# Twelve slots a window in place of fourteen, a third operand buffer, and a first pair whose preparation is spread, in a hybrid RWKV-7 and attention encoder

## The chip, the cores and the metric

The kernel runs on one core of one Trainium2 chip. The metric is the device time of one execution in microseconds (us), as the median of several runs. Engines are called by the names of the profile: PE multiplies matrices, DVE and ACT do elementwise work, POOL helps a little, SP issues the transfers. Each engine works through its own list of instructions in order and waits, where it must, for another engine's semaphore.

## The reference, cut to what matters

Two layers (DEPTH 2) over 256 tokens (T) of width 2048. In each, the normalised input goes through one projection, whose columns feed a bidirectional RWKV-7 time mixer with 16 heads of 64 and a windowed attention with 16 heads; the two, each under its own gate, go through an output projection and are added to the input.

```python
proj = jnp.einsum('btd,dc->btc', h, w_in[l])
rw_in = bidir_token_shift(rw_in, shift_mu[l])          # u + mu0*(prev-u) + mu1*(next-u)
...
kk = kk * lax.rsqrt(jnp.maximum(jnp.sum(kk * kk, -1, keepdims=True), 1e-24))
...
def step(S, inp):                                      # for each head, each direction
    r_t, w_t, k_t, v_t, kk_t, a_t = inp
    s_kk = jnp.einsum('bhvk,bhk->bhv', S, kk_t)
    S = (S * w_t[:, :, None, :] - s_kk[..., None] * (a_t * kk_t)[:, :, None, :]
         + v_t[..., None] * k_t[:, :, None, :])
    return S, jnp.einsum('bhvk,bhk->bhv', S, r_t)
...
bonus = bonus + jnp.sum(rh * kd * rkf, -1, keepdims=True)
mu = jnp.mean(y, -1, keepdims=True)                    # then variance, norm, bonus * v, gate
...
x = x + jnp.einsum('btc,cd->btd', mix, w_out[l])
```

## The kernel before, in words

**The stream.** The input projection of a layer is a stream `S` of steps. A step is three matmuls of 128x256 (L286, L287, L288): weights and input are split into a high and a low part (XH and XL for the input, `hi` by ACT at L216 and `lo` by DVE at L218 for the weights), and a step multiplies high by high, low by high and high by low. Sixteen steps make a tile of 128 columns in PSUM (`pm`), which DVE and ACT take out with the token shift (L413 to L416: `u`, `kr`, `vg`). The output projection is such a stream too, with MH and ML as its input. `S.run(n)` writes n steps; behind them weights are prepared ahead.

**The chains.** Beside the stream, the sixteen heads are worked on in eight pairs (NP = 8, `p`). The recurrence is brought into chunks of 64 tokens (NC = 4), so that it needs small matrix products. Three generators, each cut into stages by `yield`, write a pair's work:

- `scan_p` prepares: decay and learning rate by the matmuls `pza` (L648 to L650), a sum over each head of the squared key (`pk`), exponentials, the reciprocal `kd`, the operands BK and MV, and a second sum over the head for the bonus (`pbn`, of an operand `km` that has the tag `lw`). `head_sums` (L654) writes both sums; the bonus `bv` comes from the second.
- `scan_i` builds the chunks' matrices (`pg` L746, `ge` L752, AB, AL), transposes (`pt` L769 and L777, taken out by ACT as `bt` L782 and `suv` L787), and inverts a unit triangular matrix in levels: `tv` and `tt` begin as the unit matrix (L816), then `pq`, QF, `pd` and masked copies (L837 to L857), and a last step `pf`, `q`, `pn`, `vf` (L863 to L882).
- `scan_b` runs the state over the chunks: `pcc` L902, `rh` L904, L915, then `suv` by ACT L920 and DVE L927, L925, and the outputs `py` (L909 and L932). Behind the last chunk come the norm (`ysq` by ACT L943, `yv` DVE L944 and POOL L945, `ysq` with the mean removed by DVE at the helper's line L231, L952 by PE, `t` L954) and MH and ML, the operand of the output projection.

The helper at L231 writes many DVE and ACT instructions, so its line stands for many places; they are told apart by their tiles. PSUM has eight banks: two for `pm`, two (`ps_c`) for `pcc` and `py`, and two buffers of two banks that all other small products share (`pza`, `pk`, `pbn`, `pg`, `pt`, `pq`, `pd`, `pf`, `pn`).

**The windows.** A layer's projection is cut into thirteen windows of 64 steps. `window` cuts its 64 steps into SLOTS slots; in a slot it first runs the stages that tables place there (STAGE_P, STAGE_I, STAGE_B, and ATT for attention in the last windows), then its share of the stream's steps, four or five of them. A pair enters one window after another: in window `w`, `scans(w)` runs the preparation of pair w-1, the inverse of w-2 (its end in w-3's table), and the state of w-3 (its end of w-4). From window 4 to window 7 all chains are under way at once; the projection is followed by 256 steps of output projection.

**What sets the order.** On PE the order is as written: stage by stage and step by step. The other engines' lists are ordered by a scheduler from priorities (PRIO_B, PRIO_LO, and the helpers PA and PV, which put instructions in turn with the chains). Buffers are had by tag; where a tag has two buffers, the third pair's write waits for the first pair's last reader.

Of the kernel before, what the change touches and what calls it, by code (L numbers as in the profile page):

```python
# [9 lines left out]
F32 = mybir.dt.float32  # L10
F32R = mybir.dt.float32r
F16 = mybir.dt.float16
# [9 lines left out]
T = 256  # L22
DEPTH = 2
RW = 1024
NKT = D // 128
# [5 lines left out]
NC = T // CHUNK  # L31
# [9 lines left out]

SLOTS = 14
STAGE_P = [4, 5, 6, 7, 8, 9, 10, 11, 13]
STAGE_I = (list(range(SLOTS)), [0, 1])
STAGE_B = (list(range(1, 14)), [1, 2, 3, 4])
ATT = [
    [4, 11],
    [1, 3, 6, 8, 11, 13],  # L50
    [0, 2, 5, 7, 8, 10, 12, 13],
]
PRIO_B = 95
PRIO_LO = 40
# [75 lines left out]
def hybrid_trunk_kernel(ctx, tc, xT, wi, wv, wo, par, fing, dup, iup, sink, pos, cst, out):  # L130
    nc = tc.nc
    V, A, G, PE, SY = nc.vector, nc.scalar, nc.gpsimd, nc.tensor, nc.sync

    def pool(name, bufs, **kw):
        return ctx.enter_context(tc.tile_pool(name=name, bufs=bufs, **kw))
# [3 lines left out]
    wrp = pool("wrp", 3)  # L139
    wsp = pool("wsp", 2)  # L140
    sp = pool("sp", 1)
    big = pool("big", 4)
# [12 lines left out]
    def st(tag, shape, dt=F32, bufs=1):  # L155
        return sp.tile([128, *shape], dt, tag=tag, name=tag, bufs=bufs)
# [7 lines left out]
    half = (slice(0, 64), slice(64, 128))  # L164
# [9 lines left out]
    def bigt(dt, name):  # L174
        return big.tile([128, NKT, T], dt, tag="big", name=name)

    def x_split(XH, XL, x, k, l):
        g = G0[:, k : k + 1] if l == 0 else PR[:, l, P_NG + k : P_NG + k + 1]
# [45 lines left out]
    class InTurn:  # L224


        def __init__(self, engine):
            self.engine = engine
# [66 lines left out]

    first_w = wrp.tile([128, 1024], F32, tag="raw", name="raw")
    G0 = cp.tile([128, NKT], F32, name="G0")
    X0 = bigt(F32, "X0")
# [73 lines left out]

    def window(n, *gens, groups=SLOTS):

        done = 0
        for i in range(groups):
            for g, at in gens:
                for _ in range(at.count(i)):
                    if g.__name__ == "scan_b":
                        with tc.high_priority(offset=PRIO_B):  # L380
                            next(g, None)
                    else:
                        next(g, None)
            upto = n * (i + 1) // groups
            S.run(upto - done)
            done = upto
# [198 lines left out]
    def queue_output(l):  # L585

        L = layers[l]
        last = l + 1 == DEPTH

        def tile_of(k):  # L590
            xs = []

            def begin():
                xs.append(st("vg", [T], bufs=8))
                SY.dma_start(out=xs[0], in_=L.xin[:, k, :])

            def evac(pm):
                if last and k == 0:
                    L.X2 = bigt(F32, "X2")
                x = L.X2[:, k, :] if last else xs[0]  # L600
                V.tensor_tensor(x, pm, xs[0], op=ALU.add)
                to = end if last else layers[l + 1]
                if k == 0:
                    to.norm = Norm()
                    to.acc = st("acc", [T])
                    if not last:
                        to.XH, to.XL = bigt(F32R, "XH"), bigt(F32R, "XL")
# [24 lines left out]
    def layer(l):  # L632
        L = layers[l]
        prm = lambda o, j: PR[:, l, o + j : o + j + 1]
        dpm = lambda o, j: DP[:, l, o + j : o + j + 1]
        L.MH, L.ML = MH, ML = bigt(F32R, "MH"), bigt(F32R, "ML")

        def mix_split(j, y, g2):
            mf = st("mf", [T])
            V.scalar_tensor_tensor(mf, y, 0.5, g2, op0=ALU.mult, op1=ALU.mult)  # L640
            A.activation(MH[:, j, :], mf, AF.Copy)
            V.tensor_tensor(ML[:, j, :], mf, MH[:, j, :].bitcast(F32), op=ALU.subtract)

        order = (list(range(NC)), list(range(NC - 1, -1, -1)))
        cs = lambda c: slice(c * 64, (c + 1) * 64)
# [6 lines left out]
        def head_sums(o, x):  # L652
            for r in half:
                PE.matmul(o[r, 0:T], bones[r, r], x[r, 0:T], start=True, stop=True)  # L654
# [3 lines left out]
        def scan_p(p, t):  # L658
# [60 lines left out]
            PC = st("pc", [2, NC], bufs=3)  # L719
            PA.activation(PC[:, 0, :], PP[:, 0, :, 63], AF.Copy)  # L720
            PA.activation(PC[:, 1, :], PP[:, 1, :, 0], AF.Copy)
            yield


# [7 lines left out]
            t.update(BK=BK, MV=MV, PC=PC, bv=bv)  # L732
            yield


        def scan_i(p, t):
            VV, BK, MV = t["v"], t["BK"], t["MV"]
            flat = lambda x: x.rearrange("p d c j -> p (d c) j")
            GE = st("ge", [2, 2, NC, 2, 64], bufs=2)
            GE = [GE[:, h] for h in range(2)]  # L740
            GEd = lambda d: pick(GE[0], every, d * NC * 128, [2 * NC * 128, 2], [128, NC], [1, 128])
            for d in range(2):
# [30 lines left out]
            BT = st("bt", [2, 2, 3, 64], bufs=2)  # L773
            for d in range(2):
                for i in range(3):
                    for h in range(2):
# [3 lines left out]
                            ident[half[h], half[h]],  # L780
                        )
            A.activation(BT.rearrange("p h d i j -> p h (d i j)"), pt2[:, :, 0:384], AF.Copy)  # L782
            SUV = st("suv", [2, NC, 2, 64], bufs=2)
            t["SUV"] = SUV
            for h in range(2):
                for q in range(2):
# [24 lines left out]


            TC = st("tv", [2, NC, 64], F16)
            TT = st("tt", [2, NC, 64], F16)
            for x in (TC, TT):
                V.tensor_copy(flat(x), EYE.unsqueeze(1).to_broadcast([128, 2 * NC, 64]))  # L816
# [69 lines left out]
        def scan_b(p, t):  # L886
            GE, MV, BT, SUV, PC, bv = (t[n] for n in ("GE", "MV", "BT", "SUV", "PC", "bv"))


            pyt = ps_c.tile([128, 512], F32, tag="y", name="py")  # L890
            py = pyt[:, 0:256].rearrange("p (c j) -> p c j", j=64)
            for i in range(NC):
                ci = [order[d][i] for d in range(2)]

# [24 lines left out]
                for h in range(2):  # L919
                    A.activation(here(h), pc[half[h], 1], AF.Copy)  # L920
                yield
                if i < NC - 1:
# [110 lines left out]
        def attend():  # L1033

            scores(0)
            yield
            flip(0)
            scores(1)
            yield
            for j in range(8):  # L1040
                values(j)
                if j < 6:
                    scores(j + 2)
                yield
                if j < 7:
                    flip(j + 1)
                    yield

        for w in range(NP + 2):
            window(64, *scans(w), *([(setup_, [2, 5])] if l == 0 and w == 0 else []))  # L1050
        att = attend()
        window(64, *scans(NP + 2), (att, ATT[0]))
        window(64, *scans(NP + 3), (att, ATT[1]))
# [6 lines left out]
    V.memset(QF, 0.0)  # L1060
    L0 = layers[0]
    L0.norm = Norm()
    L0.XH, L0.XL = bigt(F32R, "XH"), bigt(F32R, "XL")
    for k in range(NKT):
        x_split(L0.XH, L0.XL, X0[:, k, :], k, 0)
        S.run(1)
# [113 lines left out]
```

## Time and profile before

| | |
|---|---|
| median of three runs | 1224.29 us (1222.6 to 1225.03) |
| profiled execution | 1220.4 us, span 1218.6 |
| mean granted PE clock | 0.992 |
| layer 0: projection's 13 windows | 27.77 to 518.91 us |
| layer 0: output projection | 518.91 to 623.83 us |
| layer 1: projection's 13 windows | 623.83 to 1113.19 us |
| a steady window (4 to 7 of a layer) | 42.07 us |

The windows' borders are found in the trace by counting the stream's matmuls. A row of the timeline has the start in us from the span's start, the duration, the engine, line and operation, and what is written from what. A row of the groups has the count, then the busy time and the mean of one in ns, then the idle time ahead with what ended most of it. A row of waits has the engine and line, what it waited for, and the sum, the number and the longest of the waits.

### The profile page before, as it was taken

How to read it: one execution, taken by the hardware profiler on the slowest of the kernel's cores; microseconds unless marked ns; L12 is line 12 of the kernel's file. 1: busy time of each engine (PE TensorE's matmuls, PEld its weight loads, DVE VectorE, ACT ScalarE, POOL GpSimd, SP SyncE). 2: the span in 40 equal slices, each digit the busy share in tenths (PEclk: the TensorE clock that was granted, in tenths of full speed). 3: DMA queues.
4: the chain of work that ended last, by engine and by line, in shares of the span. 5: the costliest groups of instructions: out<-in, count | busy, mean ns of one | idle time of the engine just before them, and what ended most of it. 6: DMA issues, size and time to landing. Idle time of an engine off the chain costs nothing. (4 is left out here: it accounts for less than half of the span.)

```text
span 1218.6 us, 38161 instructions
## 1 busy us (share of the span) xinstructions
PE 1177.0 (97%) x16204; PEld 1092.3 (90%) x16204; DVE 929.5 (76%) x2067; ACT 747.6 (61%) x1840; POOL 19.1 (2%) x23
## 2 busy tenths in 40 slices
PE   7989999999999999999999899999999999999996
PEld 6978998999898889999999788989999888899996
DVE  7978878888877668866677788878887866786554
ACT  6656665766666557655555556766676565675553
POOL 0000000000000000000000000000000000000000
PEclk9999999999999999999999999999999999999998
DMA  7533233323323433477654333233233334345653
GB/s 252 177 129 125 95 112 111 107 96 116 119 89 102 134 111 132 141 242 237 205 189 163 111 121 114 86 107 126 90 112 106 115 101 133 125 142 177 208 191 123
DMA packets 60411, 166.72 MB, mean 137 GB/s; under 512 B 7728, under 2 KB 22736, under 8 KB 60240
## 3 DMA queue, kind: packets, MB, share of 16 engines
q1 hardware_dynamic: 60240, 164.27, 40.5%
q8 instruction: 127, 2.08, 0.7%
q14 instruction: 44, 0.36, 0.1%
HBM read 157.43 MB, written 4.19 MB: 133 GB/s over the span
## 5 line engine op out<-in xcount | busy, mean ns | idle before, releaser
L286 PE MATMUL pm<-XH,hi 128*128 128x256 f32 x1664 | 497.0, 299 | 8.1 <-ACT XH L179 5.9
L216 ACT ACTIVATE hi<-raw 128x512 fp32r<-128x512 f32 x560 | 328.4, 624 | 247.8 <-PE pm L287 173.6
L288 PE MATMUL pm<-XH,lo 128*128 128x256 f32 x1664 | 470.1, 282 | 3.2 <-DVE lo L218 3.2
L287 PE MATMUL pm<-XL,hi 128*128 128x256 f32 x1664 | 469.7, 282 | 0.1
L218 DVE TENSOR_TENSOR lo<-raw,hi 128x512 fp32r<-128x512 f32 x560 | 368.5, 687 | 89.8 <-ACT hi L216 83.0
L286 PEld LDWEIGHTS pm<-XH,hi 128*128 128x128 f32 x1664 | 315.7, 190 | 33.8 <-issue 13.4
L288 PEld LDWEIGHTS pm<-XH,lo 128*128 128x128 f32 x1664 | 316.2, 190 | 4.5 <-DVE lo L218 4.0
L287 PEld LDWEIGHTS pm<-XL,hi 128*128 128x128 f32 x1664 | 316.5, 190 | 0.7 <-DVE XL L180 0.7
L286 PE MATMUL pm<-MH,hi 128*128 128x256 f32 x512 | 144.0, 281 | 0.0
L287 PE MATMUL pm<-ML,hi 128*128 128x256 f32 x512 | 143.8, 281 | 0.0
L288 PE MATMUL pm<-MH,lo 128*128 128x256 f32 x512 | 143.8, 281 | 0.0
L286 PEld LDWEIGHTS pm<-MH,hi 128*128 128x128 f32 x512 | 96.6, 189 | 0.8 <-issue 0.8
L287 PEld LDWEIGHTS pm<-ML,hi 128*128 128x128 f32 x512 | 96.6, 189 | 0.0
L288 PEld LDWEIGHTS pm<-MH,lo 128*128 128x128 f32 x512 | 96.6, 189 | 0.0
L920 ACT ACTIVATE suv<-pcc 64x128 f32<-64x128 f32 x128 | 34.2, 267 | 20.4 <-PE pq L847 14.4
L856 DVE CAST_PREDICATED tv<-LV,pd 128x256 f16<-128x256 uint8 x80 | 34.5, 431 | 13.6 <-PE pd L855 13.1
L849 ACT ACTIVATE QF<-pq 128x256 f16<-128x256 f32 x80 | 30.9, 386 | 20.8 <-PE pq L847 20.0
L752 DVE TENSOR_TENSOR ge<-pg,C 128x1024 f32<-128x1024 f32 x32 | 39.1, 1222 | 5.0 <-PE pg L746 5.0
L904 ACT ACTIVATE rh<-pcc 128x128 f32<-128x128 f32 x64 | 17.5, 273 | 35.3 <-PE pcc L902 34.9
L1005 ACT ACTIVATE mv<-mv,mx 128x257 f32<-128x257 f32 x64 | 31.8, 502 | 11.6 <-DVE mx L1002 11.6
L746 PE MATMUL pg<-mv,bk 64*128 64x128 f32 x512 | 37.2, 285 | 0.0
L857 DVE CAST_PREDICATED tt<-LV,pd 128x256 f16<-128x256 uint8 x80 | 34.1, 426 | 0.0
(240 smaller groups left out, 1849.9 us busy)
## 6 DMA issues: line engine op xcount, KB each, us to landing
raw<-wi SPq DMA_DIRECT2D x207, 512.0 KB, 3.4
raw<-wo SPq DMA_DIRECT2D x64, 512.0 KB, 3.8
raw<-wv SPq DMA_DIRECT2D x8, 512.0 KB, 3.2
rrot<-u SPq DMA_DIRECT2D x80, 32.0 KB, 1.9
vg<-xT SPq DMA_DIRECT2D x16, 128.0 KB, 5.2
xd<-vg SPq DMA_DIRECT2D x16, 128.0 KB, 2.4
vg<-xd SPq DMA_DIRECT2D x16, 128.0 KB, 3.5
g<-dup SPq DMA_DIRECT2D x16, 97.0 KB
```

Source lines behind the costliest of these rows:

```text
L216: A.activation(hi[:, q], raw[:, q], AF.Copy)
L218: V.tensor_tensor(lo[:, q], raw[:, q], hi[:, q].bitcast(F32), op=ALU.subtract)
L286: PE.matmul(pm, wh, rh[:, kk, :], start=(kk == 0), stop=False)
L287: PE.matmul(pm, wh, rl[:, kk, :], start=False, stop=False)
L288: PE.matmul(pm, wl, rh[:, kk, :], start=False, stop=(kk == 15))
L746: PE.matmul(pg[:, h, c * 128 : (c + 1) * 128], BK[half[h], d, c, 1 - h : 3 - h, :].rearrange("p s j -> p (s j)"), MV[half[h], d, c].rearra ...
L752: V.tensor_tensor(GEd(d), pg.rearrange("p h (c x) -> p h c x", c=NC), gm[d].unsqueeze(1).unsqueeze(1).to_broadcast([128, 2, NC, 128]), op= ...
L849: A.activation(t_sub(QF), flat4(pq[:, :, 0:128]), AF.Copy)
L856: V.copy_predicated(t_sub(TC), t_mask, flat4(pd[:, :, 0:128]))
L857: V.copy_predicated(v_sub(TT), v_mask, flat4(pd[:, 0, 128:384].rearrange("p (d x) -> p d x", d=2)))
L920: A.activation(here(h), pc[half[h], 1], AF.Copy)
L1005: A.activation(Sc[:, h, q, 0:257], Sc[:, h, q, 0:257], AF.Exp, scale=0.125, bias=mx[:, q : q + 1], accum_out=den[:, q : q + 1])
```

## The change

A window has 12 slots (of five or six steps) in place of 14, and all tables are written anew. The inverse runs over twelve slots and the first four of the next window. The state scan runs from slot 3 to 11 and then from slot 0 to 7 of the next window, where before it had 1 to 13 and 1 to 4. `scan_p` has two more yields, so that its two head sums are stages of their own, which `scans` puts ahead of the inverse in their slot (6 and 11). The first pair of a layer has tables of its own (STAGE_P0), which spread its preparation over windows 0, 1 and 2; before, all of it was in window 1. GE, BT and SUV get a third buffer, used by pairs with p % 3 == 2: it lies in the second halves of MH and ML, which are free until the last pairs. The second unit matrix (`tt`) is copied a stage later, and `py` is allocated behind the first yield of `scan_b`.

```diff
-SLOTS = 14
-STAGE_P = [4, 5, 6, 7, 8, 9, 10, 11, 13]
-STAGE_I = (list(range(SLOTS)), [0, 1])
-STAGE_B = (list(range(1, 14)), [1, 2, 3, 4])
+SLOTS = 12
+STAGE_P = (([6, 11], [4, 5, 6, 7, 8, 8, 9, 10, 11]),)
+STAGE_P0 = (([], [10, 11]), ([3], [3, 4, 5, 7, 9]), ([3], [1, 3]))
+STAGE_I = (list(range(SLOTS)), [0, 1, 2, 3])
+STAGE_B = (list(range(3, SLOTS)), list(range(8)))
...
-        L.MH, L.ML = MH, ML = bigt(F32R, "MH"), bigt(F32R, "ML")
+        L.MH, L.ML = MH, ML = Halves(F32R, "MH", "mh").more(), Halves(F32R, "ML", "ml").more()
...
+        spare = [x.half(1, F32).rearrange("p k t -> p (k t)") for x in (MH, ML)]
+        def third(p, n, tag, off, shape, dt=F32):
+            if p % 3 < 2:
+                return st(tag, shape, dt, bufs=2)
+            w = int(np.prod(shape))
+            names = " ".join(f"a{i}" for i in range(len(shape)))
+            x = spare[n][:, off : off + w]
+            return x.rearrange(f"p ({names}) -> p {names}", **{f"a{i}": v for i, v in enumerate(shape)})
...
             head_sums(pk, sq)
+            yield
...
             head_sums(pb, km)
-            bv = st("bv", [T], bufs=3)
+            yield
+            t["bv"] = bv = st("bv", [T], bufs=3)
...
-            GE = st("ge", [2, 2, NC, 2, 64], bufs=2)
+            GE = third(p, 0, "ge", 0, [2, 2, NC, 2, 64])
...
-            for x in (TC, TT):
-                V.tensor_copy(flat(x), EYE.unsqueeze(1).to_broadcast([128, 2 * NC, 64]))
-            t.update(GE=GE, BT=BT)
-            yield
+            V.tensor_copy(flat(TC), eyes)
+            t.update(GE=GE, BT=BT)
+            yield
+            TT = st("tt", [2, NC, 64], F16)
+            V.tensor_copy(flat(TT), eyes)
...
-            for lag, scan, at in ((4, scan_b, STAGE_B[1]), (3, scan_i, STAGE_I[1]), (3, scan_b, STAGE_B[0]), (2, scan_i, STAGE_I[0]), (1, scan_p, STAGE_P)):
+            prep = [(lag, at) for lag, at in enumerate(STAGE_P0) if lag == w] + [(1, at) for at in STAGE_P if w > 1]
+            stages = [(4, scan_b, STAGE_B[1]), (3, scan_i, STAGE_I[1]), (3, scan_b, STAGE_B[0])]
+            stages += [(lag, scan_p, at[0]) for lag, at in prep]
+            stages += [(2, scan_i, STAGE_I[0])]
+            stages += [(lag, scan_p, at[1]) for lag, at in prep]
```

PE's instructions stay the same in kind and number. Between stretches of the stream the small groups are fewer: 261 in place of 291 in the two layers.

The first place where the order moves is ACT's list at the start of window 5 of layer 0, from the last steps of the inverse to the transposes of the next pair (`q` and `vf` belong to the inverse, `t` and `ysq` to the norm, `bt` and `suv<-pt` to the transposes). Before:

```order
L216 ACTIVATE hi<-raw 128x512 x4
L425 ACTIVATE g<-g 128x256
L870 ACTIVATE q_3546<-pf 128x512
L954 ACTIVATE t_3584<-py,PR 128x256
L882 ACTIVATE vf<-pn 128x512
L904 ACTIVATE rh<-pcc 128x128
L216 ACTIVATE hi<-raw 128x512 x2
L920 ACTIVATE suv<-pcc 64x2x64 x2
L231 ACTIVATE AB<-ge 64x512 x2
L782 ACTIVATE bt<-pt 128x768
L787 ACTIVATE suv<-pt 64x4x64 x4
```

After, in the same window:

```order
L241 ACTIVATE hi<-raw 128x512 x2
L985 ACTIVATE ysq,yv<-py 128x64 x4
L911 ACTIVATE q_3609<-pf 128x512
L256 ACTIVATE AB<-ge 64x512 x2
L822 ACTIVATE bt<-pt 128x768
L827 ACTIVATE suv<-pt 64x4x64 x4
L241 ACTIVATE hi<-raw 128x512 x2
L439 ACTIVATE kr<-u,DP 128x256
L942 ACTIVATE rh<-pcc 128x128
L923 ACTIVATE vf<-pn 128x512
L996 ACTIVATE t_3754<-py,PR 128x256
```

The norm's squares (ysq, L985) have come in front of `q`, and AB, `bt` and `suv` follow without a state step or a weight's `hi` between them.

The second is DVE's list around the norm of the same window. Before, at the end of window 4:

```order
L231 SCALAR_TENSOR_TENSOR lw<-lw,PR,kr 128x256
L944 TENSOR_SCALAR yv<-yv 128x4
L231 TENSOR_TENSOR ysq<-py,yv 128x256
L218 TENSOR_TENSOR lo<-raw,hi 128x512 x2
L856 COPY_PREDICATED tv<-LV,pd 128x2x4x32
L857 COPY_PREDICATED tt<-LV,pd 128x2x4x32
L231 TENSOR_TENSOR bv<-pbn,vg 128x256
```

After, in window 5:

```order
L986 TENSOR_SCALAR yv<-yv 128x4
L855 COPY tv<-EYE 128x512
L438 TENSOR_TENSOR u<-pm,rb 128x256
L243 TENSOR_TENSOR lo<-raw,hi 128x512
L859 COPY tt<-EYE 128x512
L243 TENSOR_TENSOR lo<-raw,hi 128x512
L440 SCALAR_TENSOR_TENSOR kr<-u,PR,kr 128x255
L881 COPY_PREDICATED tv<-LV,pq 128x2x128
L441 SCALAR_TENSOR_TENSOR kr<-u,PR,kr 128x255
L256 TENSOR_TENSOR ysq<-py,yv 128x256
```

Between `yv` and `ysq` there now stand the unit copies, a shift's steps, two weights' `lo` and the first masked copy of the next inverse.

The third is PE's list where the second head sum stands, in window 4: slot 13 before, slot 11 after. Before:

```order
L855 LDWEIGHTS QF
L855 MATMUL pd<-tt,QF 64x32
L654 MATMUL pbn<-lw,C 64x256 x2
L286 MATMUL pm<-XH,hi 128x256
L287 MATMUL pm<-XL,hi 128x256
L288 MATMUL pm<-XH,lo 128x256
```

After:

```order
L313 MATMUL pm<-XH,lo 128x256
L967 MATMUL pcc<-suv,bt 64x64 x4
L974 MATMUL py<-suv,ge 64x64 x4
L692 MATMUL pbn<-lw,C 64x256 x2
L894 LDWEIGHTS tt
L894 MATMUL pd<-QF,tt 64x32
```

The sum now stands ahead of the inverse's `pd` in its slot, and seven slots behind `pza` instead of nine.

More of the change, by code (lines that the diff above doesn't have):

```diff
@@ L39 @@
 QG0 = 2 + 4 * 8 + 2
-SLOTS = 14
-STAGE_P = [4, 5, 6, 7, 8, 9, 10, 11, 13]
-STAGE_I = (list(range(SLOTS)), [0, 1])
-STAGE_B = (list(range(1, 14)), [1, 2, 3, 4])
+SLOTS = 12
[3 more added lines that the diff above has]
+STAGE_B = (list(range(3, SLOTS)), list(range(8)))
 ATT = [
-    [4, 11],
-    [1, 3, 6, 8, 11, 13],
-    [0, 2, 5, 7, 8, 10, 12, 13],
+    [4, 10],
+    [2, 3, 5, 7, 9, 11],
+    [0, 2, 4, 6, 7, 8, 10, 11],
 ]
@@ L141, in hybrid_trunk_kernel @@
     sp = pool("sp", 1)
-    big = pool("big", 4)
+    big = pool("big", 1)
     dram = pool("dram", 1, space=bass.MemoryType.DRAM)
@@ L172, in hybrid_trunk_kernel, with bigt, __init__, half @@
     gm = (cc("gmf"), cc("gmb"))
-    def bigt(dt, name):
-        return big.tile([128, NKT, T], dt, tag="big", name=name)
+    def bigt(dt, name, tag):
+        return big.tile([128, NKT, T], dt, tag=tag, name=name)
+    class Halves:
+        def __init__(self, dt, name, tag):
+            self.args = dt, name, tag
+            self.t = []
+        def half(self, i, dt=None):
+            d, name, tag = self.args
+            return big.tile([128, NKT // 2, T], dt or d, tag=f"{tag}{i}", name=f"{name}{i}")
+        def more(self):
+            self.t.append(self.half(len(self.t)))
+            return self
+        def __getitem__(self, at):
+            rows, k, cols = at
+            h = NKT // 2
+            if isinstance(k, slice):
+                n = k.start // h
+                return self.t[n][rows, k.start - n * h : k.stop - n * h, cols]
+            return self.t[k // h][rows, k % h, cols]
     def x_split(XH, XL, x, k, l):
@@ L297, in hybrid_trunk_kernel @@
     G0 = cp.tile([128, NKT], F32, name="G0")
-    X0 = bigt(F32, "X0")
+    X0 = Halves(F32, "X0", "ml").more().more()
     SY.dma_start(out=first_w[:, 0:512], in_=wi[0, 0, 0, :, 0:512])
@@ L598, in evac @@
                 if last and k == 0:
-                    L.X2 = bigt(F32, "X2")
+                    L.X2 = bigt(F32, "X2", "xh")
                 x = L.X2[:, k, :] if last else xs[0]
@@ L721, in scan_p @@
             PA.activation(PC[:, 1, :], PP[:, 1, :, 0], AF.Copy)
+            t.update(BK=BK, MV=MV, PC=PC)
             yield
@@ L771, in scan_i @@
                         )
-            BT = st("bt", [2, 2, 3, 64], bufs=2)
+            BT = third(p, 1, "bt", 0, [2, 2, 3, 64])
             for d in range(2):
@@ L782, in scan_i @@
             A.activation(BT.rearrange("p h d i j -> p h (d i j)"), pt2[:, :, 0:384], AF.Copy)
-            SUV = st("suv", [2, NC, 2, 64], bufs=2)
+            SUV = third(p, 1, "suv", 768, [2, NC, 2, 64])
             t["SUV"] = SUV
@@ L813, in scan_i @@
             TC = st("tv", [2, NC, 64], F16)
-            TT = st("tt", [2, NC, 64], F16)
-            for x in (TC, TT):
-                V.tensor_copy(flat(x), EYE.unsqueeze(1).to_broadcast([128, 2 * NC, 64]))
+            eyes = EYE.unsqueeze(1).to_broadcast([128, 2 * NC, 64])
+            V.tensor_copy(flat(TC), eyes)
             t.update(GE=GE, BT=BT)
             yield
+            TT = st("tt", [2, NC, 64], F16)
+            V.tensor_copy(flat(TT), eyes)
             dch = [(d, c, h) for c in range(NC) for d in range(2) for h in range(2)]
@@ L887, in scan_b @@
             GE, MV, BT, SUV, PC, bv = (t[n] for n in ("GE", "MV", "BT", "SUV", "PC", "bv"))
-            pyt = ps_c.tile([128, 512], F32, tag="y", name="py")
-            py = pyt[:, 0:256].rearrange("p (c j) -> p c j", j=64)
             for i in range(NC):
@@ L921, in scan_b @@
                 yield
+                if i == 0:
+                    pyt = ps_c.tile([128, 512], F32, tag="y", name="py")
+                    py = pyt[:, 0:256].rearrange("p (c j) -> p c j", j=64)
                 if i < NC - 1:
@@ L968, in scans @@
             gens = []
-            for lag, scan, at in ((4, scan_b, STAGE_B[1]), (3, scan_i, STAGE_I[1]), (3, scan_b, STAGE_B[0]), (2, scan_i, STAGE_I[0]), (1, scan_p, STAGE_P)):
+            prep = [(lag, at) for lag, at in enumerate(STAGE_P0) if lag == w] + [(1, at) for at in STAGE_P if w > 1]
[3 more added lines that the diff above has]
+            stages += [(lag, scan_p, at[1]) for lag, at in prep]
+            for lag, scan, at in stages:
                 p = w - lag
@@ L1050, in layer @@
             window(64, *scans(w), *([(setup_, [2, 5])] if l == 0 and w == 0 else []))
+        MH.more()
+        ML.more()
         att = attend()
@@ L1062, in hybrid_trunk_kernel @@
     L0.norm = Norm()
[L1063 removed]
+    L0.XH, L0.XL = bigt(F32R, "XH", "xh"), bigt(F32R, "XL", "xl")
     for k in range(NKT):
```

3 lines of the change are left out of this document (1 added, 2 removed).

## The prediction

> **What bounds the kernel now.** I read the busy shares first, then the windows one by one, then the waits of TensorE.
>
> ```profile
> span 1218.6 us, 38161 instructions
> PE 1177.0 (97%) x16204; PEld 1092.3 (90%) x16204; DVE 929.5 (76%) x2067; ACT 747.6 (61%) x1840; POOL 19.1 (2%) x23
> ```
>
> PE is at work for 97% of the span, so time leaves only with PE's own work or its few waits, and anything that makes PE wait is paid in full. The next view cuts the span at the windows: layer 0's windows 0 and 1, the slow piece at the end of 1, windows 2, 3 and 4, layer 1's windows 0, 1 and 2, and last a stretch of window 4 that the third wait below needs. The columns are the length, then the busy time of each engine, then the granted clock.
>
> ```profile
> 27.77:50.41 22.64, 22.64 (x193) 22.64 (x194) 20.62 (x51) 13.11 (x26) 0.00 (x0) 1.00 0.54 183
> 50.41:83.95 33.54, 27.83 (x215) 26.17 (x213) 27.53 (x58) 22.35 (x42) 0.00 (x0) 0.95 0.45 148
> 80.52:83.95 3.43, 3.43 (x18) 3.21 (x16) 0.42 (x1) 0.06 (x1) 0.00 (x0) 0.51 0.18 73
> 83.95:120.66 36.71, 35.08 (x531) 31.75 (x531) 31.34 (x61) 22.55 (x50) 0.00 (x0) 1.00 0.35 115
> 120.66:162.28 41.62, 41.55 (x739) 37.70 (x738) 34.11 (x71) 27.35 (x72) 1.01 (x1) 1.00 0.31 102
> 162.28:204.34 42.06, 41.99 (x755) 38.12 (x754) 35.13 (x75) 28.06 (x74) 1.01 (x1) 1.00 0.33 107
> 623.83:646.36 22.53, 22.53 (x195) 22.53 (x194) 16.67 (x32) 11.76 (x23) 0.00 (x0) 1.00 0.56 188
> 646.36:678.65 32.29, 27.46 (x214) 25.67 (x212) 23.79 (x44) 16.34 (x35) 0.00 (x0) 0.95 0.46 153
> 678.65:715.34 36.69, 35.06 (x533) 31.73 (x532) 31.34 (x61) 22.62 (x50) 0.00 (x0) 1.00 0.35 117
> 180.27:200.72 20.45, 20.38 (x363) 18.57 (x364) 20.00 (x43) 13.91 (x42) 0.00 (x0) 1.00 0.32 105
> ```
>
> In the steady windows (4 to 7 of a layer, here 4) PE does not wait: 41.99 of 42.06 us. Beside it DVE is busy for 35.13 us, 84%, in one strict order. Waiting is found in windows 1 and 2 alone, and these rows name it:
>
> ```profile
> PE pbn L654 <- DVE lw L231: 8.2, 2, 4.1
> PE pq L847 <- DVE tv L856: 5.8, 4, 1.6
> PE pk L654 <- ACT t L231: 1.6, 1, 1.6
> ```
>
> So the kernel is bound by PE, except where the first pair of each layer is prepared: there PE waits for the chain through ACT and DVE, and behind the 4.1 us wait the clock is 0.51 for 3.43 us.
>
> **The change part by part.** PE's instructions stay the same, so moves among windows cancel; what counts is restarts and waits.
>
> *Fewer slots.* Two stretches of projection matmuls, of four and of five steps (four and five L286 in them):
>
> ```profile
> 170.73:172.34 1.61, 1.23 (x4) 0.75 (x4) 1.00 0.11 27
> 173.33:175.29 1.96, 1.50 (x5) 0.94 (x5) 1.00 0.36 142
> ```
>
> A step is 0.35 us, so four need 1.41; the other 0.20 of 1.61 is the restart behind each group of small matmuls. By the order there are 30 groups fewer in the two layers, two in each of windows 3 to 9 and two besides: 30 x 0.20 = -6.0 us. A stretch of six steps, of which there are now four in a window, takes 2.31.
>
> *First pair spread.* In place of one window it has the end of window 0, window 1 and the start of window 2. PE's waits of window 1 are 33.54 - 27.83 = 5.71 in layer 0 and 32.29 - 27.46 = 4.83 in layer 1. The clock's loss is 3.43 x (1 - 0.51) = 1.7 at most; I take 1.6 in each, since a few of the 3.43 us are no stream. The same chain now has about twice the slots between its stages, so I let all of it go: -7.3 - 6.4 = -13.7 us. Its cover is projection work; gone, it would be 0.
>
> *Head sums ahead, two more yields, eye copy a stage later, later py tile.* No work by itself; they count through the waits that follow, as does the third buffer, which takes away the reason for a write to GE, BT or SUV to wait for the pair two before (not a wait in the rows above, so 0). No queue of SP's or POOL's is passed: no DMA is moved ahead of another in the steady windows, and POOL's one instruction a pair (1.01 us) is ready long before its reader.
>
> *A new wait at slot 3.* State update, its output matmuls (py), ysq, the inverse's last step (pf, q) and the transposes of the next pair (pt) now fall together. In the order ACT has, from the end of py: ysq x4, q, AB x2, bt, suv x4, with nothing between. Before, these lie in slots 0, 2 and 12. PE's four rows of groups with the row behind each, then ACT's:
>
> ```profile
> 162.28 0.30 PE L863 MATMUL pf<-tv,NEYE 64*64 64x256 f16 x4
> 162.79 1.16 PE L746 MATMUL pg<-mv,bk 64*128 64x128 f32 x16
> 165.84 0.30 PE L876 MATMUL pn<-tt,EYE 64*64 64x256 f16 x2
> 166.53 1.16 PE L746 MATMUL pg<-mv,bk 64*128 64x128 f32 x16
> 169.78 0.27 PE L769 MATMUL pt<-C,vg 64*64 64x64 f32 x1
> 170.73 0.38 PE L286 MATMUL pm<-XH,hi 128*128 128x256 f32 x1
> 172.95 0.33 PE L837 MATMUL pq<-tv,AB 64*64 64x32 f16 x10
> 173.33 0.38 PE L286 MATMUL pm<-XH,hi 128*128 128x256 f32 x1
> ```
>
> ```profile
> L943 ACT ACTIVATE ysq<-py 128x64 f32<-128x64 f32 x4 | 0.8, 226 | 0.9 <-PE py L932 0.9
> 163.63 0.58 ACT L870 ACTIVATE q<-pf 128x512 f16<-128x512 f32 x1
> 170.91 1.28 ACT L231 ACTIVATE AB<-ge 64x512 f16<-64x512 f32 x2
> 172.22 0.81 ACT L782 ACTIVATE bt<-pt 128x768 f32<-128x768 f32 x1
> 173.04 1.55 ACT L787 ACTIVATE suv<-pt 64x256 f32<-64x256 f32 x4
> 174.94 1.14 ACT L216 ACTIVATE hi<-raw 128x512 fp32r<-128x512 f32 x2
> ```
>
> ACT needs 0.80 + 0.55 + 1.30 + 0.82 + 1.55 = 5.0, and 0.1 to start. The level-1 matmuls behind it (pq) write into the PSUM buffer that suv<-pt is read from, so they wait for its last row. Until then PE has pf 0.51 (162.28 to 162.79), pn with L902 0.62 (165.84 to 166.53 less the few L952 among them), pt 0.90 (169.78 to 170.73 less L915's) and a stretch of six, 2.31: 4.3. Wait 0.8 us. Bounds: 0, if q and AB are done ahead of py's end, to 1.4.
>
> *A second at slot 4.* The mean-removed output goes ysq (DVE) to the L952 matmuls, two slots behind py's end, and DVE does eight things first, the lo's of which need hi's that stand behind suv<-pt on ACT.
>
> ```profile
> L218 DVE TENSOR_TENSOR lo<-raw,hi 128x512 fp32r<-128x512 f32 x16 | 10.5, 685 | 1.6 <-ACT hi L216 1.5
> L415 DVE SCALAR_TENSOR_TENSOR kr<-u,PR,kr 128x255 f32<-128x255 f32 x2 | 1.0, 482 | 0.2 <-ACT kr L414 0.2
> L856 DVE CAST_PREDICATED tv<-LV,pd 128x256 f16<-128x256 uint8 x5 | 2.2, 431 | 0.8 <-PE pd L855 0.8
> 174.70 0.42 DVE L413 TENSOR_TENSOR u<-pm,rb 128x256 f32<-128x256 f32 x1 [0.60 <-PE pm L288]
> 167.16 0.29 DVE L816 COPY tt<-EYE 128x512 f16<-128x512 f16 x1
> ```
>
> First hi done 5.0 + 0.6 = 5.6 behind py's end; then lo 0.65, tt 0.2, lo 0.6, kr, tv, kr 1.2 together, ysq 0.4: 8.7. PE is there after 5.1 + level 1 (172.95 to 173.33) 0.38 + a stretch of five 1.96 = 7.5. Wait 1.2 us, between 0 and 1.6.
>
> *A third at slots 10 and 11.* The second head sum (pbn) ends the preparation that begins with pza.
>
> ```profile
> 177.32 0.28 PE L650 MATMUL pza<-XA,iu 96*128 96x256 f32 x1
> 201.79 0.41 PE L654 MATMUL pbn<-lw,C 64*64 64x256 f32 x2
> 180.27 0.45 DVE L856 CAST_PREDICATED tv<-LV,pd 128x256 f16<-128x256 uint8 x1 [0.82 <-PE pd L855]
> 200.24 0.48 DVE L231 SCALAR_TENSOR_TENSOR lw<-lw,PR,kr 128x256 f32<-128x256 f32 x1
> ```
>
> Before, pbn comes 24.3 us behind pza, nine slots, and its operand (lw, 200.24) ends 1.1 us ahead of it; DVE has worked from 180.27 without a gap (20.00 busy in the 20.45 of the windows' last row). Now pbn comes seven slots behind pza and first in its slot: 37 steps (13.0 us), seven restarts (1.3) and the small groups of six slots (6.7) make 21.0 us. DVE's list between the first state update behind pza and lw, counted in the order with the durations above, is some 20.6 us (nine lo 5.4, reciprocal 1.7, six state updates 1.7, six tv and tt 2.0, four shift steps 1.6, the rest 8.2), begins 2.3 behind pza, and so ends at 22.9. Wait 1.8 with the start, with 0.5 at the level before it: I take 2.2, between 1.0 and 2.7.
>
> *Sum.* A steady window waits 0.8 + 1.2 + 2.2 = 4.2, near the middle of the bounds: eight of them +33.6. Window 3 has part of it (3.3), 8 and 9 the ends (1.0 and 0.8): 2 x 5.1 = +10.2. Window 2, with the first pair's late pbn, waits by the same walk 4.7 in place of the 1.63 of before (36.71 - 35.08): 2 x 3.1 = +6.2. With -6.0 and -13.7 that is +30.3: 1220.4 us of the profiled execution become 1250.7. The runs' median (1224.3) stands 3.9 above that execution, so 1254.
>
> **The rivals.**
>
> *The covers hold.* The other side. ACT's and DVE's queues stand full only where PE runs ahead; if q and AB are through before py ends, the first two waits vanish, and if DVE drops the gaps it has (7 us a steady window) the third too. Price: -6.0 - 13.7 = -19.7, with window 2's waits gone -23: 1201 to 1205. For it: ACT is busy 28 of 42 us. Against it: DVE's stretch without a gap. It decides where the new waits are under 39% of those priced (19.7 of 50.0), some 1.6 us in a steady window.
>
> *Half the waits.* A wait early in a window gives DVE time for the later one. With 25 in place of 50: +5.3, 1230.
>
> *The clock.* After a 1.6 us wait (window 2) the row says 1.00, after 4.1 it says 0.51, so no wait priced here should touch it. If several waits near each other did, one loss of 1.6 in each of twelve windows adds 19: 1273. [...]
>
> *The first pair doesn't gain.* Its waits move to windows 1 and 2 in full: +13.7, 1268. Against it stands the doubled cover.
>
> **How the numbers follow.** Likeliest, three waits in the steady window: 0.61, with its own range 1238 to 1268. Half the waits 0.17, covers hold 0.15, clock 0.03, first pair 0.04. About 0.2%, 2.4 us, is what a measurement of this kernel can tell from no change. Half the waits spreads over 1218 to 1240, so 0.02 of it is faster and 0.04 the same. Faster 0.17, same 0.04, slower 0.79. A range from 1222 to 1270 leaves out the covers' case with its neighbours and the clock, 0.20.
>
> **What would show it.** Right: the steady windows are 45 to 47 us long, with three waits of PE in each, at level 1 for ACT's suv, at the output's mean (L994 now) for DVE's ysq, and at pbn (L692 now) for DVE's lw; windows 0 and 1 together are near 48 us with no row of 0.51. Wrong: steady windows near 41.6 us (covers hold), rows of 0.5 in windows 3 to 9 (clock), or a 4 us wait still in windows 1 or 2 (first pair). The step most open is the third wait, a difference of two long sums: 1 us less of DVE's list takes 8 to 10 us off the forecast.

## The result and the profile after

The changed kernel takes 1270.35 us (median, 1267.26 to 1271.3) against 1224.49: ratio 1.0373, 95% interval 1.0352 to 1.0394. It is slower by 46 us, where 30 were forecast; the time lies 0.35 us above the stated range. The profiled execution took 1271.3 us. Its page, span and busy time:

```profile
span 1269.5 us, 38164 instructions
PE 1179.0 (93%) x16204; PEld 1101.8 (87%) x16204; DVE 933.1 (74%) x2067; ACT 747.3 (59%) x1840; POOL 19.7 (2%) x23
```

PE's work is the same (1179.0 against 1177.0), the span is 50.9 us longer: nearly all that came is waiting. The same cut into windows as before, for layer 0: windows 0, 1, 2, 4, 5 and 8, and layer 1's 0 and 1 (length, busy time by engine, granted clock):

```profile
28.12:52.62 24.50, 24.50 (x204) 24.46 (x205) 22.27 (x55) 14.94 (x31) 0.00 (x0) 1.00 0.51 175
52.62:80.92 28.30, 25.74 (x199) 24.61 (x197) 24.57 (x51) 20.20 (x37) 0.00 (x0) 0.94 0.48 156
80.92:119.80 38.88, 34.70 (x488) 31.76 (x487) 31.62 (x62) 21.93 (x48) 0.00 (x0) 1.00 0.38 128
164.22:211.31 47.09, 41.95 (x756) 38.46 (x755) 35.62 (x74) 28.11 (x73) 1.01 (x1) 1.00 0.30 96
211.31:259.67 48.36, 43.38 (x755) 39.82 (x754) 35.80 (x74) 28.12 (x73) 1.01 (x1) 0.96 0.29 93
354.96:397.54 42.58, 41.69 (x755) 38.38 (x754) 33.55 (x70) 26.91 (x70) 1.01 (x1) 1.00 0.29 92
650.17:674.39 24.22, 24.22 (x206) 24.22 (x205) 18.11 (x34) 13.76 (x28) 0.00 (x0) 1.00 0.53 175
674.39:698.70 24.31, 23.54 (x199) 22.84 (x197) 20.67 (x39) 15.04 (x32) 0.00 (x0) 1.00 0.55 182
```

By windows, over both layers, the difference of the spans is: 0 and 1 together -9.7, 2 +4.3, 3 +5.6, the eight steady ones +44.9, 8 and 9 -0.3, 10 to 12 +4.5, the rest +1.6. In layer 0's window 1 PE waits 2.3 us for a weight's `hi`, and the clock is 0.50 for 3.41 us behind it (the 0.94 of the second row). The waits of PE in window 5 are three causes in four rows:

```profile
PE pq L888 <- DVE tv L897: 1.8, 2, 1.5
PE py L994 <- DVE ysq L256: 1.2, 1, 1.2
PE pbn L692 <- DVE lw L256: 1.1, 1, 1.1
PE pq L878 <- ACT suv L827: 0.9, 1, 0.9
```

They are the three that the prediction named. The first, on ACT's list (window 5; the start, the duration, and in brackets PE's wait):

```profile
219.55 0.23 ACT L985 ACTIVATE ysq<-py 128x64 f32<-128x64 f32 x1
220.36 0.61 ACT L911 ACTIVATE q<-pf 128x512 f16<-128x512 f32 x1
220.84 1.28 ACT L256 ACTIVATE AB<-ge 64x512 f16<-64x512 f32 x2
222.13 0.81 ACT L822 ACTIVATE bt<-pt 128x768 f32<-128x768 f32 x1
222.95 1.55 ACT L827 ACTIVATE suv<-pt 64x256 f32<-64x256 f32 x4
224.55 0.33 PE L878 MATMUL pq<-tv,AB 64*64 64x32 f16 x11 [0.87 <-ACT suv L827]
```

From ysq to the end of suv 4.95 us without a gap, 5.0 forecast; PE waits 0.87 behind it, 0.8 forecast. The third, on DVE's list (PE's `pd`, then DVE, then PE):

```profile
246.26 0.40 PE L896 MATMUL pd<-tt,QF 64*64 64x32 f16 x16
246.84 0.68 DVE L256 SCALAR_TENSOR_TENSOR th<-th,kd 128x512 f32<-128x512 f32 x1
247.55 0.42 DVE L438 TENSOR_TENSOR u<-pm,rb 128x256 f32<-128x256 f32 x1
247.89 0.68 DVE L256 SCALAR_TENSOR_TENSOR bk<-th,ip 128x512 f32<-128x512 f32 x1
248.49 0.69 DVE L256 TENSOR_TENSOR lw<-lw,kr 128x512 f32<-128x512 f32 x1
249.09 0.48 DVE L440 SCALAR_TENSOR_TENSOR kr<-u,PR,kr 128x255 f32<-128x255 f32 x1
249.49 0.69 DVE L256 TENSOR_TENSOR bk<-lw,ip 128x512 f32<-128x512 f32 x1
250.09 0.48 DVE L441 SCALAR_TENSOR_TENSOR kr<-u,PR,kr 128x255 f32<-128x255 f32 x1
250.48 0.42 DVE L897 CAST_PREDICATED tv<-LV,pd 128x256 f16<-128x256 uint8 x1
250.95 0.30 PE L888 MATMUL pq<-tv,AB 64*64 64x32 f16 x16 [1.50 <-DVE tv L897]
255.14 0.59 DVE L969 TENSOR_TENSOR ML<-pcc,pc 64x128 f32<-64x128 f32 x2 [0.78 <-PE pcc L967]
255.76 0.48 DVE L256 SCALAR_TENSOR_TENSOR lw<-lw,PR,kr 128x256 f32<-128x256 f32 x1
```

PE's `pd` is done at 246.7, and the masked copy `tv` of it, needed two groups on, stands behind seven instructions of the next pair's preparation and the shift: 3.8 us. The head sum's operand `lw` comes at the end of the same list. In this window DVE also waits 0.78 us on PE at a state update (L969) ahead of it; that wait is found in windows 5 and 7 of both layers, where the clock drops, and not in 4 and 6. There PE waits for `lw` all the same, 1.3 us in place of 0.9 to 1.1, so it is the list and not this wait that makes `lw` late.

Last, the clock: the wait on `tv` and the 3.45 us behind it, in window 5 and then in window 4 (PE's busy time, clock), and two more rows of window 5, cut where the clock changes:

```profile
249.45:250.95 1.50, 0.00 (x1) 1.00 0.13 49
250.95:254.40 3.45, 3.45 (x32) 0.59 0.14 21
202.34:203.85 1.51, 0.01 (x1) 1.00 0.18 71
203.85:207.30 3.45, 2.90 (x47) 1.00 0.14 27
248.17:251.58 3.41, 1.91 (x43) 1.00 0.36 141
251.58:254.99 3.41, 3.41 (x25) 0.50 0.26 66
```

The same wait of 1.5 us is followed by half the clock in windows 5 and 7 and not in 4 and 6, in both layers (0.96 over the windows with it, 1.00 over the others); the windows with it are 1.1 to 1.3 us longer.

### The profile page after: what moved, and what is told of

It is laid out like the page before. It is cut to its first block, busy times and chain, and to the rows that moved or that the text cites. A ratio compares the mean times of both kernels' runs of the same rounds, so it can differ in the third digit from the quotient of the medians.

```text
span 1269.5 us, 38164 instructions
## 1 busy us (share of the span) xinstructions
PE 1179.0 (93%) x16204; PEld 1101.8 (87%) x16204; DVE 933.1 (74%) x2067; ACT 747.3 (59%) x1840; POOL 19.7 (2%) x23
## 5 line engine op out<-in xcount | busy, mean ns | idle before, releaser
L888 PE MATMUL pq<-tv,AB 64*64 64x32 f16 x1280 | 32.7, 185 | 24.8 <-DVE tv L897 23.9
L888 PEld LDWEIGHTS <-AB 64*64 64x64 f16 x1280 | 25.0, 106 | 31.9 <-issue 25.6
L958 ACT ACTIVATE suv<-pcc 64x128 f32<-64x128 f32 x96 | 25.9, 269 | 32.7 <-PE pcc L953 20.9
L438 DVE TENSOR_TENSOR u<-pm,rb 128x256 f32<-128x256 f32 x52 | 21.6, 418 | 29.5 <-PE pm L313 29.2
L1052 ACT ACTIVATE mv<-mv,mx 128x257 f32<-128x257 f32 x64 | 31.9, 500 | 14.0 <-DVE mx L1049 13.7
L969 DVE TENSOR_TENSOR suv<-pcc,pc 64x128 f32<-64x128 f32 x72 | 20.6, 286 | 21.9 <-PE pcc L967 21.3
```

The costliest lines, as they stand in the source:

```text
L438: V.tensor_tensor(u, pm, L.norm.rb, op=ALU.mult)
L888: PE.matmul(narrow(pq[:, d], h ^ d, c), hq(AB, d, c, h), sub(TC, h, d, c, d * b), start=True, stop=True)
L969: V.tensor_tensor(here(h, i + 1), pS[half[h]], pick(PC, half[h], i, [2 * NC - 1 - 2 * i, 2], [0, 64]), op=ALU.mult)
L1052: A.activation(Sc[:, h, q, 0:257], Sc[:, h, q, 0:257], AF.Exp, scale=0.125, bias=mx[:, q : q + 1], accum_out=den[:, q : q + 1])
```

## The experiments

Times are medians; the kernel before took 1222.6 to 1224.5 us beside them. Theories: (T) the loss is made of separate waits, each of which comes from the place of a stage in the tables, and the first pair's spread is a gain beside it; rivals: (R1) there is too little room on DVE and ACT, so that a wait that is removed comes back elsewhere; (R2) another part of the change (third buffer, split head sums, spread) costs by itself.

**The spread alone, on 14 slots.** Only the first pair's tables, with what they need (BK, MV and PC are handed on a stage earlier):

```diff
+STAGE_P0 = ([12, 13], [4, 5, 6, 8, 11], [1, 4])
...
+prep = [(lag, scan_p, at) for lag, at in enumerate(STAGE_P0) if lag == w] + [(1, scan_p, STAGE_P)] * (w > 1)
-... (1, scan_p, STAGE_P)):
+... *prep):
```

> The kernel before with 14 slots and all its tables, the first pair's preparation alone spread over windows 0, 1 and 2. Theory (the first pair's waits and the clock loss behind them go, windows 4 to 7 stay 42.1 us): 10 to 14 us faster than before, 1210 to 1215 us, no PE row of waits over 2 us in windows 0 to 2. Rival (the waits only move into window 2): 1222 to 1227 us.

Measured: 1213.13 us, ratio 0.9924 (0.9909 to 0.9938). Layer 0's windows 1 and 2:

```profile
52.67:78.73 26.06, 24.45 (x199) 23.05 (x197) 24.22 (x51) 20.73 (x37) 0.00 (x0) 1.00 0.50 170
78.73:116.53 37.80, 35.60 (x534) 31.83 (x534) 32.84 (x65) 22.32 (x50) 0.00 (x0) 1.00 0.37 128
```

The 4.1 us wait and the piece at clock 0.51 are gone. A part comes back: in window 1 waits of 0.7 + 0.5 for weights, in window 2 0.6 + 0.3 that were not there. So 9.5 us are won and not 13.7.

**The change without the spread.**

```diff
-prep = [(lag, at) for lag, at in enumerate(STAGE_P0) if lag == w] + [(1, at) for at in STAGE_P if w > 1]
+prep = [(1, at) for at in STAGE_P]
```

> The changed kernel, but the first pair is prepared like all others, in window 1. Theory (the parts add): the spread's 8 to 12 us come on top of the change's 1270, so 1278 to 1282 us, and windows 4 to 7 stay at 47 to 48 us. Rival (with 12 slots the first pair's chain is covered either way): within 3 us of 1270.

Measured: 1279.13 us, ratio 1.0458 (1.0435 to 1.0480), 8.8 above the changed kernel; in window 1 a wait on pbn of 4.6 us is back. The parts add. It also showed the clock: windows 4 and 5 now are

```profile
167.35:215.56 48.21, 43.38 (x756) 39.82 (x755) 35.80 (x74) 28.12 (x73) 1.01 (x1) 0.96 0.27 93
215.56:262.67 47.11, 41.92 (x756) 38.44 (x755) 35.63 (x74) 28.13 (x73) 1.01 (x1) 1.00 0.29 95
```

with the same waits (1.8 for `tv`, 1.2 for ysq, 1.0 and 1.3 for pbn, 0.8 and 0.9 at level 1): 0.96 and 1.00 here, where the changed kernel has 1.00 in window 4 and 0.96 in window 5. The same work with the same waits is found with the loss and without it.

**The rest of the change, on 14 slots.** Spread, split and forward head sums, third buffer and later copy of `tt`, with the slots and tables of before:

```diff
-SLOTS = 12
+SLOTS = 14
-STAGE_P = (([6, 11], [4, 5, 6, 7, 8, 8, 9, 10, 11]),)
+STAGE_P = (([6, 13], [4, 5, 6, 7, 8, 9, 10, 11, 13]),)
...   # STAGE_I, STAGE_B, ATT as before, STAGE_P0 in proportion
```

> The changed kernel with 14 slots and the tables of before: what is left of the change is the spread, the split and forward head sums, the third buffer and the later copy of tt. Theory (all that was lost is lost by the number of slots and the tables that follow from it): as the spread alone, 1211 to 1216 us, steady windows 42.1 us. Rival (head sums ahead of the inverse's step, or the third buffer in MH and ML, cost by themselves): 1218 us or more.

Measured: 1213.52 us, ratio 0.9907 (0.9884 to 0.9930); window 5 is 42.08 us long and PE waits for nothing in it. This is the spread alone (1213.13) within the error, so the other parts together cost nothing with 14 slots. The whole loss of 57 us (1270.4 against 1213.5) lies with 12 slots and the tables that go with them.

**The third buffer.**

```diff
-            if p % 3 < 2:
+            if True:
```

> The changed kernel without its third buffer: GE, BT and SUV rotate over two, as before. Theory (with 12 slots a pair's operands live into slot 7 of the fourth window after, so that the third pair's ge in slots 0 to 2 must wait for the first pair's last state step): a wait of several us at ge and behind it at pt in every window from 4 on, 1300 us or more. Rival (the readers of the first pair are through in time, and the third buffer buys nothing): within 3 us of 1270.

Measured: 1310.34 us, ratio 1.0692 (1.0662 to 1.0722): 40 us slower than the changed kernel. Window 4 has new rows:

```profile
PE pf L904 <- DVE ge L792: 1.4, 1, 1.4
PE pg L786 <- DVE tt L898: 0.9, 1, 0.9
PE pt L809 <- DVE ge L792: 0.7, 1, 0.7
```

The third buffer takes these waits away. They cost by the clock too: its mean is 0.970 here and 0.988 in the changed kernel, which by estimate is up to 24 of the 40 us ((0.988 - 0.970) x 1310).

**The head sum later.** A test of the third wait: pbn and the step behind it in slot 1 of the next window.

```diff
-STAGE_P = (([6, 11], [4, 5, 6, 7, 8, 8, 9, 10, 11]),)
+STAGE_P = (([6], [4, 5, 6, 7, 8, 8, 9, 10]), ([1], [1]))
...   # scans(w) takes the second entry for the pair before
```

> The changed kernel with the second head sum (pbn) and the step behind it moved from slot 11 to slot 1 of the next window, nothing else. Theory (pbn is late because its place is seven slots behind pza): its wait of 0.9 to 1.3 us goes in windows 2 to 7 of both layers, the 1.5 us wait on tv one slot earlier stays; 12 to 14 us off, 1256 to 1258 us, and 3 to 6 less if the clock's loss goes too. Rival (DVE has too little time in the window, wherever pbn stands): the wait comes back at tv or in the next window, 1266 to 1270 us.

Measured: 1263.10 us, ratio 1.0334 (1.0317 to 1.0352): 7 us off, between the theories. Window 5:

```profile
PE pq L888 <- DVE tv L897: 1.8, 2, 1.5
PE py L994 <- DVE ysq L256: 1.2, 1, 1.2
PE pq L878 <- ACT suv L827: 0.9, 1, 0.9
PE pg L786 <- DVE tt L898: 0.5, 1, 0.5
```

pbn's row is gone, the other three stand, and a new one of 0.5 has come. The windows that lose the clock (2 to 5 in layer 0, 5 to 7 in layer 1, each at 0.96) are seven, where the changed kernel has four among its steady ones; without that the gain would be some 4 us larger (an estimate: three windows more at 1.1 to 1.3 us). So T for the wait, with a part for R1.

**The state scan later.** A test of the first two waits: the norm's squares no longer fall into the slot of the transposes.

```diff
-STAGE_B = (list(range(3, SLOTS)), list(range(8)))
+STAGE_B = (list(range(4, SLOTS)), list(range(9)))
```

> The changed kernel with the state scan one slot later (slots 4 to 11, then 0 to 8 of the next window), nothing else, so that the norm's squares fall one slot behind the transposes and the norm's product one slot later. Theory (the first two waits come from the norm standing in the same slot as the inverse's end and the transposes): the 0.9 us wait at level 1 shrinks to under 0.2 and the 1.2 us wait at the output's mean goes, 2.0 us in each of windows 4 to 7 and 0.9 in 8 and 9, together about 19 us: 1250 to 1254 us. Rival (what is won there is waited for at tv and pbn, since DVE's list is the limit): 1262 to 1270 us.

Measured: 1248.97 us, ratio 1.0219 (1.0204 to 1.0234), 21 us off and 1 us under the range that T gave. Window 5, 45.34 us long at clock 1.00:

```profile
PE pq L888 <- DVE tv L897: 1.6, 2, 0.9
PE pq L878 <- ACT suv L827: 0.6, 1, 0.6
PE pd L894 <- ACT QF L890: 0.5, 1, 0.5
PE pbn L692 <- DVE lw L256: 0.5, 1, 0.5
```

The wait for ysq is gone, and pbn's is half. The level-1 wait fell only from 0.9 to 0.6, not under 0.2. Most of the norm's 0.8 us on ACT had been covered by `pf`: `q` began 0.41 us behind PE's last `pf` and now begins 0.25 behind it, since a state update's copies (L958, 0.57 us) have come in front. `suv` is ready 0.15 us earlier, counted from there, and PE comes 0.14 later. In the steady windows no wait is over 0.9 us, and the clock is 1.00 in all of them.

**A shorter list.** The third wait again, by DVE's load and not by a table:

```diff
-            PV.reciprocal(KD, pk[:, 0:T])
+            PV.tensor_scalar(KD, pk[:, 0:T], 0.0, 1e-4, op0=ALU.mult, op1=ALU.add)
```

> The changed kernel with the 1.76 us reciprocal of each pair's preparation replaced by a 0.4 us operation on the same tile (this leaves out the key's norm: a constant stands in its place). Theory (the third wait, tv and pbn together 2.8 to 3.1 us in a window, is DVE's list between pza and pbn, which is too long for seven slots): 1.3 us less of list takes 1.3 to 1.5 us off in each of windows 4 to 7 and about 1 in 2 and 3, 14 to 16 us, and up to 6 more if the clock's loss goes: 1248 to 1256 us. Rival (the wait comes from where tv stands in the list, not from its length): under 4 us off, 1266 to 1270.

Measured: 1255.03 us, ratio 1.0259 (1.0236 to 1.0282), 15 us off, for a kernel that leaves out the key's norm. tv's wait in window 5 is 1.0 in place of 1.8 in sum, pbn's 1.3 in place of 1.1, and windows 5 to 7 keep their clock at 1.00 (3 and 4 of layer 0 are at 0.93 and 0.99, with waits no longer than 1.3 us); window 5 is 46.44 in place of 48.36. Window 6, at 1.00 in both kernels, went from 47.08 to 46.42: of the 1.3 us saved in the list half arrives. From the state update behind pza to the end of `lw` DVE takes 21.2 us there in place of 21.9, since in the shorter list it waits 0.94 us for ACT's `iuh`, where it waited 0.16 and 0.31 for ACT. The length of the list counts, as T has it; a part comes back as a wait for ACT, as R1 has it. The rest of the 15 us is mostly clock by estimate (its mean is 0.993 here and 0.988 in the changed kernel, (0.993 - 0.988) x 1256 = 6), so that the total fell into T's range is in part luck.

**The preparation earlier.** One stage in each slot from 3 to 10, the head sum in the next window; then the same with the state scan later.

```diff
-STAGE_P = (([6, 11], [4, 5, 6, 7, 8, 8, 9, 10, 11]),)
+STAGE_P = (([5], [3, 4, 5, 6, 7, 8, 9, 10]), ([1], [1]))
...   # scans(w) as in the run with the head sum later
-STAGE_B = (list(range(3, SLOTS)), list(range(8)))        # second kernel only
+STAGE_B = (list(range(4, SLOTS)), list(range(9)))
```

> The changed kernel with the preparation one slot earlier (slots 3 to 10, one stage in each), and the second head sum in slot 1 of the next window. Theory (the third wait is a list too long for its slots): tv's wait of 1.5 falls under 0.5 and pbn's is gone, 2.5 to 3 us in each of windows 4 to 7, and the clock stays 1.00; the first two waits stay or grow by up to 0.5 where ACT and DVE have more to do in slots 3 and 4: 1240 to 1250 us. Rival (DVE's load of the window has no room anywhere): the first two waits grow by what the third loses, 1258 to 1266.

> The same, and the state scan a slot later too (slots 4 to 11, then 0 to 8). Theory (three waits with three causes, each of which a table moves): what is left is 0.6 us at level 1 and about 0.5 at tv in a window of 41.6: 1213 to 1225 us. Rival (the causes are one, too little room on DVE and ACT): windows stay above 44 us, 1238 to 1246.

Measured: 1282.32 us (ratio 1.0487, 1.0448 to 1.0527) and 1273.30 us (1.0419, 1.0396 to 1.0442). Both expectations failed, theory and rival. Of the first, window 5 and its waits:

```profile
213.43:261.33 47.90, 44.64 (x756) 40.88 (x755) 35.45 (x74) 27.92 (x73) 1.01 (x1) 0.93 0.28 94
PE pza L686 <- ACT vf L923: 1.9, 1, 1.9
PE pq L878 <- ACT suv L827: 0.9, 1, 0.9
PE pg L786 <- DVE tt L898: 0.5, 1, 0.5
```

The third wait is gone, as expected; so is the one for ysq, which was expected to stay. But `pza` in slot 3 takes the PSUM buffer that `vf` is read from, and `vf` stands on ACT behind suv<-pt and four instructions more: a wait of 1.9 us that I had not looked for, close behind another of 0.9, and the clock at 0.93 in every steady window (PE is busy for 44.5 to 44.8 us in place of the 41.9 of a window of the changed kernel at 1.00). At full clock window 5 would be some 45.2 us by estimate (47.90 less 2.7), less than the 47.1 of the changed kernel: the waits became fewer, and the clock cost more than that. In the second kernel windows 4 to 6 are 47.0 us at 0.96, with a wait of 2.0 for `vf`. T's causes hold, but a table that cures one makes another.

**Thirteen slots.** The norm's squares, the inverse's end and the transposes in slots 0, 1 and 2, the head sum eight slots behind pza; then that with pbn in the next window.

```diff
-SLOTS = 12
+SLOTS = 13
-STAGE_I = (list(range(SLOTS)), [0, 1, 2, 3])
-STAGE_B = (list(range(3, SLOTS)), list(range(8)))
+STAGE_I = (list(range(SLOTS)), [0, 1, 2])
+STAGE_B = (list(range(2, SLOTS)), list(range(6)))
-STAGE_P = (([6, 11], [4, 5, 6, 7, 8, 8, 9, 10, 11]),)
+STAGE_P = (([6, 12], [4, 5, 6, 7, 8, 9, 10, 11, 12]),)     # first kernel
+STAGE_P = (([6], [4, 5, 6, 7, 8, 9, 10, 11]), ([1], [1]))  # second kernel
...   # STAGE_P0 and ATT in proportion; scans(w) of the second as above
```

> The changed kernel with 13 slots, tables in proportion: the norm's squares in slot 0, the inverse's end in 1, the transposes in 2, the second head sum eight slots behind pza. Theory (three causes in the tables): the first two waits go, the third has some 22.7 us for a list of some 22.5 and falls to 0 to 1 us; half the restarts are saved and the spread's 9.5: 1208 to 1220 us. Rival (the third buffer or the split head sums cost by themselves, whatever the slots): over 1235 us.

> Thirteen slots, and the second head sum in slot 1 of the next window. Theory (with 13 slots pbn is the one wait left in windows 2 to 7, 0.8 to 1.7 us each, and its list gets the room of two more slots): steady windows 41.8 us, 11 to 13 us under the 13-slot kernel: 1206 to 1210 us. Rival (as with 12 slots, where the move brought 7 of 13 us, a tt or tv behind it is late instead): 1211 to 1216 us.

Measured: 1219.45 us (ratio 0.9970, 0.9957 to 0.9982) and 1206.22 us (0.9848, 0.9829 to 0.9867). In window 4 of the first one wait is left; the second has none, and its window 5 is 41.84 us long:

```profile
PE pbn L692 <- DVE lw L256: 0.9, 1, 0.9
198.90:240.74 41.84, 41.76 (x755) 38.11 (x755) 34.92 (x74) 28.25 (x74) 1.01 (x1) 1.00 0.33 108
```

This is the fastest kernel here, 18 us under the kernel before and 64 under the changed one: the spread, the third buffer and the split head sums, with one slot more than the change has and the last sum moved across the border. Of its 7 us under the kernel with 14 slots and all else, some 3.6 by estimate are clock: its mean is 0.992 there and 0.995 here, (0.995 - 0.992) x 1212.

## What of the prediction held, and which steps failed

*Direction and mechanism.* Three waits in a steady window, at the places named. The runs that move pbn, the state scan or the preparation take away the wait they were aimed at, wholly or in part, and the one that shortens DVE's list shortens the third. The rival "the covers hold" is out. What failed is the size: +30.3 forecast on the profiled execution, +50.9 measured. The steps that failed most are the level ahead of pbn, priced at 0.5 us, where the changed kernel waits 1.8 for `tv` (1.5, and 0.3 at the level before), and the sentence that no wait priced here should touch the clock, where it is halved for 3.41 us in every second steady window. By the terms:

- *First wait*, 0.8 forecast: 0.8 to 0.9. *Second*, 1.2: 1.2. Both terms held.
- *Third wait*, 2.2: 2.8 to 3.2 (tv 1.8, pbn 0.9 to 1.3). I gave 0.5 to the level before pbn; tv alone stands behind seven instructions there. DVE's list, too, was counted short: in window 4 it takes 21.9 us from the state update to the end of `lw` (186.02 to 207.89, 21.1 of them busy), 20.6 counted. +6 us over eight windows. The bounds, 1.0 to 2.7, left out what was measured.
- *The clock*, a rival at 0.03, held in part: every second steady window loses 1.1 to 1.3 us, +5 us. It was left out because of one wait of 1.6 us with the clock at 1.00; in the trace after, a wait of 1.5 us is followed by 1.00 in window 4 and by 0.50 in window 5.
- *Restarts*, -6.0. The price of a group held: 13 slots without a wait take 41.84 us a window, 14 take 42.08, 0.24 for one group. But window 4 less its 5.1 us of waits is 42.0, not the 41.7 of 42.06 less 0.4, so about 0.3 is lost again. A part comes with the waits: the stretch with the 1.23 us wait takes 3.25 in place of 1.96, 0.06 more than the wait. The rest is not shown. +3 us.
- *First pair*, -13.7: windows 0 and 1 gained 9.7, and the spread alone is worth 9.5 by the one run and 8.8 by the other. Windows 0 and 1 together are 52.8 us in layer 0, not near 48, with the wait of 2.3 us for `hi` and the half clock behind it; in layer 1 they are 48.5. +4 us.
- *Windows 10 to 12*, taken as 0: +4.5. In layer 0 PE is busy for 1.7 us more there and 1.0 less in 8 and 9, so most of this is work that moved. PE's waits in them grew by 0.5 only: the last pair's norm (1.5 us for ysq in window 11, as the state scan now ends in slot 7 and not 4) came in place of 1.0. The sentence that waiting is found in windows 1 and 2 alone had passed over this 1.0 and 2.0 us in window 9. (The one on POOL doesn't hold before the change either: DVE waits up to 1.2 us for `yv` in a window. No such wait is left after it in the steady windows of layer 0.)
- *Windows 2, 3, 8 and 9*, +16.4, with their share of restarts taken off 14.0: +9.6, so -4 us; the ends of the pipeline wait less than I took.

With the +1.6 of the rest these make some 20 of the 20.6 us that were missed. Errors of both signs stand in the sum, so that 1270 came near the range's end says little of its parts.

## What to carry to other kernels

Where one engine's order is written by hand and the others follow it in order, a stage's place sets not only its cover but what stands ahead of its helpers in their lists: before slots are cut, sum the list of each helper from one PE group to the next, compare it with the slots between, and do so for every operand in the list, not for the last alone. Cut in small steps and test the parts alone: here 12 slots cost 57 us, 13 with one stage moved across the border won 7 over 14 (some 3.6 of them by the clock, by estimate), and the part that gained by itself (the first pair's spread) was hidden under the loss. When a table cures one wait, look at once for whose PSUM buffer the moved stage takes. And read the clock beside the waits: with the preparation earlier, PE waits 3.3 us in window 5 where it waits 5.0 in the changed kernel, and the kernel is 12 us slower, with 0.93 in every steady window where the changed kernel has 1.00 and 0.96 in turn.

## What the runs showed of the hardware that I had not expected

In the changed kernel a wait of PE of 1.5 us (for `tv`, 249.45 to 250.95 in window 5) was followed by a clock of 0.50 for 3.41 us (251.58 to 254.99); behind the same wait in window 4 (202.34 to 203.85) the clock stayed at 1.00. The state scan later, with no wait over 0.9 us in the steady windows, had 1.00 in all of them; the preparation earlier, with waits of 0.8 to 1.0 and of 1.9 us in each, had 0.93 in all of them.

How much PE worked around the wait does not tell windows 4 and 5 apart. In the changed kernel the pieces at 0.50 in windows 5 and 7 of the two layers begin at 251.58, 347.15, 869.39 and 964.96 and last 3.41 us each; in the 3.41 us ahead of them PE is busy for 1.91, 1.87, 1.92 and 1.88 us. The stretch that lies in the same way about the wait in window 4 (201.06 to 204.47) has 1.90 us of work, and the 3.41 us behind it are at 1.00. The wait of 2.3 us for `hi` in window 1 is no different: it is followed by 0.50 in the changed kernel (67.26 to 70.67), and with the short reciprocal, where a wait of 2.3 us for `hi` is found too, window 1 is at 1.00 throughout. What decides between the two is not shown by these runs.
